# Keys of both kv heads in one transpose, doubled over the partitions by their stores (hybrid attention and convolution block, one core)

## The chip, the cores and the metric

The kernel runs on one core of one Trainium2 chip. The metric is the device time of one execution in microseconds. Shown with the kernel are three timed runs and one execution taken by the hardware profiler. Engines are named as in the profile: PE is TensorE's matmul, PEld its weight load, DVE is VectorE, ACT is ScalarE, POOL is GpSimd, and SP is SyncE, which issues the DMAs.

## What is computed

One encoder layer over two sequences (256 and 2048 tokens), each with the same 16 meta tokens in front. Every token row is normalised, multiplied with one input matrix, and the columns go two ways: a windowed attention with 8 query heads and 2 key/value heads, and a gated convolution. Both are gated, concatenated, multiplied with the output matrix and added to the input. What the change touches is the key part:

```python
h = rmsnorm(z, norm_w)
proj = jnp.einsum('bld,de->ble', h, w_in)
q, k, v, g_att, c_val, c_glu, g_conv = jnp.split(proj, SPLIT_IDX, axis=-1)
q = rmsnorm(q.reshape(B, L, N_HEADS, HEAD_DIM), q_norm_w)
k = rmsnorm(k.reshape(B, L, N_KV_HEADS, HEAD_DIM), k_norm_w)      # 2 heads of 64
att = windowed_gqa(q, k, v, sink).reshape(B, L, W_ATT) * jax.nn.silu(g_att)
cnv = conformer_conv(c_val, c_glu, conv_w, conv_b, ln_w, ln_b) * jax.nn.silu(g_conv)
return z + jnp.einsum('ble,ed->bld', jnp.concatenate([att, cnv], axis=-1), w_out)
```

In the attention a block of 128 queries sees its own block of keys, the two neighbours and the meta keys; the first and the last block of a sequence have one neighbour.

## The kernel before

Tokens come in 18 blocks of 128 (two of the short sequence, sixteen of the long one) and one small block of the 16 meta tokens, called block -1. Products run in single-pass fp32 (F32R) with each operand split into a high and a low part, so one product is three matmuls.

**Projection.** The input matrix is cut into 11 units of 256 columns, the tokens into 6 groups of 384 (400 with the meta tokens). Groups 0 to 2 form the first chunk and 3 to 5 the second. Within a chunk the units run in a fixed order: convolution, its gate, attention gate, then keys and values (unit 8), then queries (units 6 and 7). So keys are made twice, once for blocks -1 to 8 and once for blocks 9 to 17. `c_group` and `g_group` multiply by `proj_et` (L863); `kv_group` and `q_group` by `proj_te` (L879), where 24 matmuls of 256 columns fill one PSUM tile named `pj`. Results that the attention needs go to DRAM: `kd` and `kmd` (keys), `vd`, `qd`, `gd`, `cd`.

**One key block** (`kv_block`). ACT squares and sums the keys of each head, POOL makes the inverse root `rk`, DVE multiplies (`kn`, L1037). The score product later wants the 64 rows of a head twice, in partitions 0 to 63 and again in 64 to 127, since the queries `q2` stand there as high part and low part (`q_split`, L403 to L406). Before, DVE writes each head twice side by side, so `kn` has 256 columns, and PE transposes each head's 128 columns by itself (L1048, two transposes into one PSUM tile `kt`). ACT scales to the high part of `ks` (L1055, 256 columns), DVE makes the low part (L1056, 256 columns), and one store writes `ks` to `kd`.

**Attention.** `load_k` brings the keys of one block's window into one of two tiles `kw`: five DMAs for an inner block, one for a first or last block (L300). `scores` multiplies `q2` with `kw` (S, L383); then bias and maximum on DVE (L441), the exponential on ACT (L453), the normalisation on POOL, transposes (L499), the product with the values (O, L533) and the output projection (y, L609). The first blocks' attention steps are spread through the last query units (`spread`), where a query block is first copied out of PSUM by ACT (`qr`, L1004), squared (`sqq`, L980), and multiplied on DVE much later (L1010); its buffer comes free when its store to `qd` has landed.

**What sets the order.** Steps are written out by a clock of ticks: `later(k, f)` runs `f` after k ticks, `store` issues a DMA two ticks later, and convolution steps on DVE (L946) are drawn by a credit of time. Beneath that a scheduler places the instructions of each engine by its own cost table, except in stretches that are marked manual (POOL from the opening of the attention, PE too after the last query block). All DMAs are issued by SP, in order. Each carries one of eight completion semaphores in turn, and its issue waits for the DMA that carried the same one, eight issues before.

Of the kernel before, what the change touches and what calls it, by code (L numbers as in the profile page):

```python
# [18 lines left out]
P = 128  # L19
D = 1024  # L20
ND = D // P
NM = 16
# [77 lines left out]
def hymba_kernel(  # L100
# [19 lines left out]
    kd = dram.tile([P, 2, KV, TOK], F32, name="kd")  # L120
    kmd = dram.tile([P, 2, KV, NM], F32, name="kmd")
# [15 lines left out]
    km = const.tile([P, 2, KV, NM], F32R, name="km")  # L137
# [56 lines left out]
    def store(dst, src):  # L194
        later(2, lambda: nc.sync.dma_start(dst, src))
# [59 lines left out]
    def attention_open():  # L255
# [10 lines left out]
        for i in range(2):  # L266
            kw.append(ap.tile([P, 2, KV, KW], F32R, tag=f"kw{i}", name=f"kw{i}", bufs=1))
# [27 lines left out]
    def load_k(b):  # L295
        t = kw[b % 2].bitcast(F32)
        at = P * (b - 1)
        if kind(b) != "in":
            at += P * (kind(b) == "first")
            nc.sync.dma_start(t[:, :, :, CC:MB], kd[:, :, :, at : at + 2 * P])  # L300
            return
        nc.sync.dma_start(t[:, :, :, CC:LB], kd[:, :, :, at + P : at + 2 * P])
        nc.sync.dma_start(t[:, :, :, LA:MA], kd[:, :, :, at : at + QC])
        nc.sync.dma_start(t[:, :, :, LB:RA], kd[:, :, :, at + QC : at + P])
        nc.sync.dma_start(t[:, :, :, RA:MB], kd[:, :, :, at + 2 * P : at + 2 * P + QC])
        nc.sync.dma_start(t[:, :, :, RB:KW], kd[:, :, :, at + 2 * P + QC : at + 3 * P])
# [103 lines left out]
    def scores(b, kv, n):  # L410
# [13 lines left out]
        for hl_k in range(2):  # L424
# [4 lines left out]
                kw[b % 2][:, hl_k, kv, c0:c1],  # L429
# [271 lines left out]
    if True:  # L701
# [321 lines left out]
        def kv_block(ws, g, o, rows, b):  # L1023
# [8 lines left out]
            kn = sp.tile([P, KV, 2, HD], F32, tag="kn", name=f"kn{b}")  # L1032
            owe(800)

            def fin():
# [3 lines left out]
                    pk.unsqueeze(2).to_broadcast([rows, KV, 2, HD]),  # L1039
                    rk[:rows, :KV].unsqueeze(2).unsqueeze(3).to_broadcast([rows, KV, 2, HD]),  # L1040
# [4 lines left out]
            def fin2():  # L1045
                pt = psum.tile([P, 512], F32, tag="d", name=f"kt{b}")
                for kv in range(KV):
                    nc.tensor.transpose(  # L1048
                        pt[:, P * kv : P * kv + rows],
                        kn[:rows, kv].rearrange("p a e -> p (a e)"),  # L1050
                        ident[:rows, :rows],
                    )
                ks = sp.tile([P, 2, KV, P], F32R, tag="ks", name=f"ks{b}")
                pr = pt[:, : 2 * P].rearrange("p (a n) -> p a n", n=P)[:, :, :rows]
# [265 lines left out]
```

## Time and profile before

| | us |
|---|---|
| three timed runs | 948.51, 948.61, 950.12 |
| median | 948.61 |
| the profiled execution | 947.32 |
| its span in the profile | 945.3 |
| PE busy in it | 938.1 |
| DVE, ACT, POOL busy | 748.8, 424.1, 296.7 |

Times in the profile count from the span's start. A row of a timeline has the start, the length, the engine, the line, the operation with its tiles, the count and, in brackets, idle time before it with what ended it. The length of a PE row is modelled to its drain, so rows overlap; the step from one start to the next is what a matmul takes of PE.

### The profile page before, as it was taken

What the parts mean: (1) busy time and instruction counts of PE and PEld (TensorE: products, weight loads), DVE (VectorE), ACT (ScalarE), POOL (GpSimd) and SP (SyncE); (2) the same over time, 40 slices, a digit from 0 to 9 for tenths busy, and PEclk for the clock granted to TensorE, in tenths of its full rate; (3) what the DMA queues carried; (4) which work ended last, traced back from release to release, by engine and by line L of the source; (5) the groups of instructions that cost most, each with busy time, mean ns of one, the idle gap of its engine ahead of it and who ended that gap; (6) DMA issues with size and microseconds to landing.
All of it is one profiled execution on the core that took longest, in us unless ns stands there. A gap on an engine that the chain in (4) does not pass through costs nothing.

```text
span 945.3 us, 16681 instructions
## 1 busy us (share of the span) xinstructions
PE 938.1 (99%) x5813; PEld 887.7 (94%) x5813; DVE 748.8 (79%) x1263; ACT 424.1 (45%) x1160; POOL 296.7 (31%) x490
## 2 busy tenths in 40 slices
PE   8999999999999999999999999999999999999998
PEld 8999999999999999999999999988888888888887
DVE  5579999997987879999995655687777677767763
ACT  7432022253457751011111456566666566656661
POOL 4310000183478400000000453755433243333332
PEclk9999999999999999999999999999999999999999
DMA  8585345686556595223333496985666556655512
GB/s 305 169 275 193 134 176 176 222 277 236 159 187 190 187 328 175 89 111 135 140 130 123 138 353 189 398 260 156 197 188 174 152 162 192 187 164 143 165 64 67
DMA packets 148659, 176.49 MB, mean 187 GB/s; under 512 B 40704, under 2 KB 111184, under 8 KB 148448
## 3 DMA queue, kind: packets, MB, share of 16 engines
q1 hardware_dynamic: 148576, 175.43, 57.4%
q8 instruction: 46, 0.75, 0.3%
q14 instruction: 37, 0.30, 0.1%
HBM read 112.69 MB, written 62.70 MB: 186 GB/s over the span
## 4 chain that ended last, share of the span: by engine, by line
PE 85%; DMA 5%; DVE 4%; SPq 2%; POOL 1%; ACT 1%; issue 1%; DVEq 0%; POOLq 0%; ACTq 0%
PE pj L863 41%; PE y L609 21%; PE pj L879 8%; PE O L533 5%; PE S L383 4%; PE pT_c L499 2%; PE pT_m L499 2%; PE pT_x L499 1%; DMA kw<-kd 1%; DMA qd<-qr 1%; DVE xt L772 1%; DVE y L946 1%; PE qT L383 1%; DMA cd<-zn 1%; DMA wraw<-in_w_in 1%
## 5 line engine op out<-in xcount | busy, mean ns | idle before, releaser
L863 PE MATMUL pj<-xh,ws 128*128 128x384 f32 (+1 forms) x1536 | 395.9, 338 | 0.1
L946 DVE SCALAR_TENSOR_TENSOR y<-us,cw,y 128x1167 f32<-128x1167 f32 x240 | 329.0, 1428 | 0.4
L863 PEld LDWEIGHTS pj<-xh,ws 128*128 128x128 f32 x1536 | 280.0, 188 | 0.4 <-ACT xh L1116 0.4
L863 PE MATMUL pj<-xl,ws 128*128 128x384 f32 (+1 forms) x768 | 260.8, 340 | 0.1
L609 PE MATMUL y<-wo,rest 128*128 128x512 f32 (+1 forms) x672 | 173.2, 395 | 0.0
L879 PE MATMUL pj<-ws,xh 128*128 128x256 f32 (+1 forms) x880 | 165.8, 284 | 0.9 <-ACT sqq L980 0.5
L863 PEld LDWEIGHTS pj<-xl,ws 128*128 128x128 f32 x768 | 144.1, 188 | 0.5 <-DVE xl L801 0.4
L879 PEld LDWEIGHTS pj<-ws,xh 128*128 128x128 f32 (+1 forms) x880 | 136.5, 187 | 2.3 <-ACT sqq L980 0.8
L609 PEld LDWEIGHTS y<-wo,rest 128*128 128x128 f32 x672 | 117.5, 189 | 21.7 <-DVE rest L566 0.3
L879 PE MATMUL pj<-ws,xl 128*128 128x256 f32 (+1 forms) x440 | 124.3, 283 | 0.0
L441 DVE CUSTOM_DVE_ANT_0 sb<-S,bias,vec 128x304 f32<-128x304 f32 (+5 forms) x144 | 74.4, 517 | 32.2 <-PE S L383 31.4
L453 ACT ACTIVATE sb<-sb,nm 128x304 f32<-128x304 f32 (+5 forms) x144 | 77.8, 541 | 48.9 <-DVE nm L441 48.2
L971 ACT ACTIVATE go<-pj 128x384 f32<-128x384 f32 x48 | 23.5, 490 | 149.8 <-PE pj L863 138.3
L879 PEld LDWEIGHTS pj<-ws,xl 128*128 128x128 f32 (+1 forms) x440 | 82.2, 187 | 0.2
L561 POOL TENSOR_TENSOR at<-at,ga 128x256 f32<-128x256 f32 x36 | 26.5, 735 | 164.8 <-DVE at L555 105.1
L479 POOL TENSOR_SCALAR sb<-sb,es 128x304 f32<-128x304 f32 (+5 forms) x144 | 73.1, 526 | 16.0 <-DVE es L466 13.2
L148 POOL TENSOR_SCALAR ssk<-ssk 128x2 f32<-128x2 f32 x18 | 7.5, 419 | 213.1 <-ACT sqk L985 211.1
L383 PEld LDWEIGHTS S<-kw,q 128*128 128x128 f32 x288 | 53.2, 188 | 11.3 <-issue 0.3
L383 PE MATMUL S<-kw,q 128*128 128x304 f32 (+5 forms) x288 | 62.7, 299 | 0.2 <-issue 0.2
L148 POOL TENSOR_SCALAR ssq<-ssq 128x4 f32<-128x4 f32 (+2 forms) x55 | 26.4, 479 | 96.5 <-ACT xn L726 73.6
L906 ACT ACTIVATE sg<-pj 128x384 f32<-128x384 f32 (+1 forms) x24 | 11.8, 492 | 83.1 <-PE pj L863 66.1
L609 PE MATMUL y<-wo,mch 128*128 128x512 f32 x144 | 47.2, 409 | 0.0
(139 smaller groups left out, 1317.7 us busy)
## 6 DMA issues: line engine op xcount, KB each, us to landing
wd<-ws SPq DMA_DIRECT2D x36, 512.0 KB, 6.0
ws<-wd SPq DMA_DIRECT2D x36, 512.0 KB, 6.0
wraw<-in_w_in SPq DMA_DIRECT2D x52, 256.0 KB, 6.4
xn<-in_z SPq DMA_DIRECT2D x18, 512.0 KB, 5.5
gd<-go SPq DMA_DIRECT2D x48, 192.0 KB, 2.1
yo<-in_z SPq DMA_DIRECT2D x36, 256.0 KB, 3.9
out_y<-yo SPq DMA_DIRECT2D x35, 256.0 KB, 2.6
wo<-wod SPq DMA_DIRECT2D x16, 512.0 KB, 7.5
```

The lines of the kernel that those rows point to most:

```text
L148: nc.gpsimd.tensor_scalar(src, src, scale, eps, op0=ALU.mult, op1=ALU.add)
L383: r = f(*a, **k)
L441: nc.vector.tensor_tensor_reduce(out=sb[:, n, c0:c1], in0=ps[:, 0:w], in1=cst["bias"][:, kv, at + c0 : at + c1], scale=1.0, scalar=nsnk[:, ...
L453: nc.scalar.activation(sb[:, n, c0:c1], sb[:, n, c0:c1], AF.Exp, bias=nm[:, n : n + 1], scale=-1.0, accum_out=rs[:, n : n + 1],)
L479: nc.gpsimd.tensor_scalar(sb[:, k, a0:a1], sb[:, k, a0:a1], es[:, k : k + 1], 1.0, op0=ALU.mult, op1=ALU.mult)
L499: nc.tensor.transpose(pt[: c1 - c0, n, :], sbt[b, kv][:, n, c0:c1], ident)
L533: nc.tensor.matmul(opj[b, kv][:, n0:n1], t[:r, kv, :], p[:r, n0:n1], start=(k == "c" and i == 0), stop=(k == "x" and i == len(work) - 1),)
L561: nc.gpsimd.tensor_tensor(at[:, pr, :], at[:, pr, :], gat[b][:, pr, :], op=ALU.mult)
L609: nc.tensor.matmul(ps, mh[mi][:, e % 4, :], wo[e, wi][:, cols], start=(e == 4 and k == 0), stop=(e == 3 and k == 2),)
L863: nc.tensor.matmul(ps[:, :n], ws[:, d, wi, P * half_i : P * half_i + P], x[xi][:, d, o : o + n], start=(k == 0), stop=(k == 3 * ND - 1),)
L879: nc.tensor.matmul(ps[:rows, :UW], x[xi][:, d, o : o + rows], ws[:, d, wi, :], start=(k == 0), stop=(k == 3 * ND - 1),)
L946: nc.vector.scalar_tensor_tensor(y[:, yo + o0 : yo + o1], u[:, o0 + k : o1 + k], cw[:, j, k : k + 1], y[:, yo + o0 : yo + o1], op0=ALU.mul ...
```

## The change

The two heads of a key block are left side by side, 128 columns in all, and one transpose turns both: head 0 lands in partitions 0 to 63 and head 1 in 64 to 127. ACT and DVE then work on 128 columns instead of 256, for the meta block on 16 instead of 32. The doubling over the partitions is done by the store: one store per head, which reads 64 partitions of `ks` twice, by a stride of zero, and writes both halves of the DRAM tile. For that `kd` has a layout by block, in which a partition's row holds a head's high and low part side by side; `kw` and `km` swap their two middle dimensions to fit, and the first and last blocks of a sequence load their two key blocks with two DMAs.

```diff
-    kd = dram.tile([P, 2, KV, TOK], F32, name="kd")
-    kmd = dram.tile([P, 2, KV, NM], F32, name="kmd")
+    kd = dram.tile([NB, P, KV, 2, P], F32, name="kd")
+    kmd = dram.tile([P, KV, 2, NM], F32, name="kmd")
...
         t = kw[b % 2].bitcast(F32)
-        at = P * (b - 1)
         if kind(b) != "in":
-            at += P * (kind(b) == "first")
-            nc.sync.dma_start(t[:, :, :, CC:MB], kd[:, :, :, at : at + 2 * P])
+            at = b - (kind(b) == "last")
+            for k in range(2):
+                nc.sync.dma_start(t[:, :, :, CC + P * k : CC + P * k + P], kd[at + k])
             return
-        nc.sync.dma_start(t[:, :, :, CC:LB], kd[:, :, :, at + P : at + 2 * P])
+        nc.sync.dma_start(t[:, :, :, CC:LB], kd[b])
...
-                kw[b % 2][:, hl_k, kv, c0:c1],
+                kw[b % 2][:, kv, hl_k, c0:c1],
...
-            kn = sp.tile([P, KV, 2, HD], F32, tag="kn", name=f"kn{b}")
+            kn = sp.tile([P, KV, HD], F32, tag="kn", name=f"kn{b}")
...
                 nc.vector.tensor_tensor(
                     kn[:rows],
-                    pk.unsqueeze(2).to_broadcast([rows, KV, 2, HD]),
-                    rk[:rows, :KV].unsqueeze(2).unsqueeze(3).to_broadcast([rows, KV, 2, HD]),
+                    pk,
+                    rk[:rows, :KV].unsqueeze(2).to_broadcast([rows, KV, HD]),
                     op=ALU.mult,
                 )
...
+                nc.tensor.transpose(pt[:, :rows], kn[:rows].rearrange("p a e -> p (a e)"), ident[:rows, :rows])
+                ks = sp.tile([P, 2 * P], F32R, tag="ks", name=f"ks{b}")
+                nc.scalar.mul(ks[:, :rows], pt[:, :rows], kscale[:, 0:1])
+                nc.vector.scalar_tensor_tensor(
+                    ks[:, rows : 2 * rows], pt[:, :rows], kscale[:, 0:1], ks[:, :rows], op0=ALU.mult, op1=ALU.subtract
+                )
+                to = (kmd if b < 0 else kd[b]).rearrange("(h p) k l n -> p h k (l n)", h=2)
                 for kv in range(KV):
-                    nc.tensor.transpose(
-                        pt[:, P * kv : P * kv + rows],
-                        kn[:rows, kv].rearrange("p a e -> p (a e)"),
-                        ident[:rows, :rows],
-                    )
-                ks = sp.tile([P, 2, KV, P], F32R, tag="ks", name=f"ks{b}")
-                pr = pt[:, : 2 * P].rearrange("p (a n) -> p a n", n=P)[:, :, :rows]
-                nc.scalar.mul(ks[:, 0, :, :rows], pr, kscale[:, 0:1])
-                nc.vector.scalar_tensor_tensor(
-                    ks[:, 1, :, :rows], pr, kscale[:, 0:1], ks[:, 0, :, :rows], op0=ALU.mult, op1=ALU.subtract
-                )
-                store(
-                    kmd if b < 0 else kd[:, :, :, P * b : P * b + P], ks[:, :, :, :rows].bitcast(F32)
-                )
+                    part = ks[HD * kv : HD * kv + HD, : 2 * rows].bitcast(F32)
+                    store(to[:, :, kv, :], part.unsqueeze(1).to_broadcast([HD, 2, 2 * rows]))
```

The lines after `fin2` stand five lower in the changed file (the transpose is L1047, ACT's scaling L1049, DVE's low part L1050). The cost table knows the shorter instructions, so the scheduler places others anew around the keys and up to the end of the last query unit.

On PE, in the second chunk's key unit, before: `pj` is the projection's PSUM tile, `kt` the transposed keys of one block, x2 a row of two equal instructions.

```order
L879 MATMUL pj_5439<-ws_8_4916,xl_3485 128x256
L879 MATMUL pj_5439<-ws_8_4916,xh_3484 128x256 x2
L879 MATMUL pj_5439<-ws_8_4916,xl_3485 128x256
L1048 MATMUL kt_5430<-ident,kn_5370 128x128 x2
L879 MATMUL pj_5439<-ws_8_4916,xh_3484 128x256 x2
L879 MATMUL pj_5439<-ws_8_4916,xl_3485 128x256
```

The same place on PE in the changed kernel:

```order
L879 MATMUL pj_5437<-ws_8_4916,xl_3485 128x256
L879 MATMUL pj_5437<-ws_8_4916,xh_3484 128x256 x2
L879 MATMUL pj_5437<-ws_8_4916,xl_3485 128x256
L1047 MATMUL kt_5429<-ident,kn_5368 128x128
L879 MATMUL pj_5437<-ws_8_4916,xh_3484 128x256 x2
L879 MATMUL pj_5437<-ws_8_4916,xl_3485 128x256
```

One of the pair is gone; it is so in all 18 blocks and in the meta block, and nothing is added on PE.

On ACT, where the first attention block's queries are prepared, before: `qr_9` is a query block on its way out of PSUM, `zn` the layer norm of the convolution, `q_0` the split queries that the first scores read.

```order
L243 ACTIVATE zn_5914<-lnu_5965,vec 128x128 x4
L1004 COPY qr_17_6139<-pj_6114 128x256
L1004 COPY qr_9_6191<-pj_6166 128x256
L243 ACTIVATE zn_5974<-lnu_6024,vec 128x128 x4
L403 CAST q_0_6040<-qT_6035 64x4x4x32
L404 CAST q_0_6040<-qT_6035 64x4x4x32
```

The same place on ACT in the changed kernel:

```order
L1004 COPY qr_17_6141<-pj_6116 128x256
L243 ACTIVATE zn_5915<-lnu_5966,vec 128x128 x4
L243 ACTIVATE zn_5975<-lnu_6025,vec 128x128 x4
L403 CAST q_0_6041<-qT_6036 64x4x4x32
L404 CAST q_0_6041<-qT_6036 64x4x4x32
L1004 COPY qr_16_6067<-pj_6042 128x256
L980 ACTIVATE sqq_16_6070<-pj_6042 128x256
L980 ACTIVATE sqq_17_6144<-pj_6116 128x256
L243 ACTIVATE zn_6034<-lnu_6079,vec 128x128 x4
L1004 COPY qr_9_6193<-pj_6168 128x256
```

The copy of `qr_9` stood ahead of the two casts of `q_0`, and now stands seven instructions behind them (the four of `zn` share a row).

On SP, near the end of the query units, before: `kw` is a key load of an end block, `qd<-qr_9` the store of that query block.

```order
L329 DMA q_6717<-qd 128x512
L364 DMA ga_6753<-gd 128x4x128
L300 DMA kw_5835<-kd 128x4x256
L195 DMA qd<-qr_9_6191 128x256
L195 DMA qd<-qr_10_6245 128x256
```

The same place on SP in the changed kernel:

```order
L329 DMA q_6720<-qd 128x512
L364 DMA ga_6756<-gd 128x4x128
L300 DMA kw_5835<-kd 128x4x128 x2
L195 DMA qd<-qr_9_6193 128x256
L360 DMA wo_6581<-wod 128x1024
```

Ahead of the store of `qr_9` there are two key loads of half the size in place of one.

12 lines of the change are left out of this document (6 added, 6 removed).

## The prediction

> **What bounds the kernel now.** I read the page first, the span and the engines' busy time.
>
> ```profile
> span 945.3 us, 16681 instructions
> PE 938.1 (99%) x5813; PEld 887.7 (94%) x5813; DVE 748.8 (79%) x1263; ACT 424.1 (45%) x1160; POOL 296.7 (31%) x490
> ```
>
> PE never rests: 7.2 us of the span are idle on it (945.3 less 938.1). So the time is the sum of PE's steps and its few stalls; work taken from DVE or ACT is worth nothing by itself. The profiled execution took 947.32 us, its span is 945.3, so 2.0 us lie outside. I make the sum against 947.32 and carry the difference to the median of the runs, 948.61.
>
> Next, what PE waits for: the view of waits on PE, less its two rows of the first 30 us, which the change doesn't reach.
>
> ```profile
> PE pj L879 <- ACT sqq L980: 0.5, 1, 0.5
> PE pj L879 <- DVE qs L1010: 0.3, 1, 0.3
> PE S L383 <- issue: 0.2, 1, 0.2
> ```
>
> Three stalls, all in the query units just behind the keys. Then the stages, as busy time by windows (start and end; PE, PEld, DVE, ACT, POOL; granted clock, DMA share, GB/s):
>
> ```profile
> 220.00:245.00 25.00, 25.00 (x213) 24.53 (x212) 23.68 (x39) 9.30 (x48) 10.67 (x18) 1.00 0.58 190
> 570.00:586.00 16.00, 15.85 (x136) 15.67 (x135) 7.76 (x20) 10.52 (x29) 6.13 (x14) 1.00 0.48 158
> 586.00:604.00 18.00, 18.00 (x153) 17.82 (x151) 9.88 (x33) 9.62 (x32) 11.90 (x25) 1.00 1.03 360
> 615.00:945.00 330.00, 327.18 (x1825) 282.13 (x1824) 237.70 (x617) 196.87 (x508) 127.42 (x215) 1.00 0.56 162
> ```
>
> The clock is full everywhere. In the first chunk's key unit (220 to 245) DVE is nearly full too; from 586 to 604 the DMA engines are. From 615 on PE is busy 327.18 of 330 us, in an order that the change leaves alone: what is won before 615 moves the end.
>
> **The transposes: the main term.** What the key blocks cost now is shown by the view of the tile `kt` (count; shortest, median, longest in ns), and what one transpose takes of PE by a place where one stands alone between projection matmuls (timeline of PE):
>
> ```profile
> L1048 PE MATMUL kt<-ident,kn x36: 270/272/300, 233.7 to 546.0; 128*128 128x128 f32 x36
> ...
> 285.05 0.28 PE L879 MATMUL pj<-ws,xh 128*128 128x256 f32 x1
> 285.17 0.27 PE L221 MATMUL lnt<-ident,y 128*128 128x128 f32 x1
> 285.20 0.36 PE L879 MATMUL pj<-ws,xh 128*128 128x256 f32 x1
> 285.40 0.28 PE L879 MATMUL pj<-ws,xl 128*128 128x256 f32 x1
> ```
>
> A `pj` hands over after 0.12 (285.05 to 285.17). From the `pj` before the transpose to the second behind it are 0.35 us (285.05 to 285.40), of which two steps of `pj` are 0.24: the transpose costs 0.11. A pair of `kt`:
>
> ```profile
> 528.95 0.29 PE L879 MATMUL pj<-ws,xh 128*128 128x256 f32 x1
> 529.07 0.38 PE L1048 MATMUL kt<-ident,kn 128*128 128x128 f32 x2
> 529.21 0.37 PE L879 MATMUL pj<-ws,xh 128*128 128x256 f32 x1
> 529.41 0.28 PE L879 MATMUL pj<-ws,xl 128*128 128x256 f32 x1
> ```
>
> 0.46 less 0.24 is 0.22, again 0.11 each: a pair has no share that a single one keeps. 36 become 18, and the meta block's two become one: 19 times 0.11 is **2.09 us** off PE, which nothing hid. The bounds are this and 0.2 more: half a hundredth of rounding for each, and the meta block's unlike shape.
>
> The Trainium skill ("TensorE: Matmul & The Clock Gate", Part 4: PE-mode transpose) gives about 275 ns for a transpose within a kernel, mostly access latency. The row of `kt` has the same 272 ns, but as the length of an instruction and not as its step; taken as the price, the skill's figure would make 5.2 us of the 19 instead of 2.1; the steps of 0.11 speak against reading it so.
>
> **DVE and ACT.** The nearest rows for 128 columns are the value split's, beside the keys' (count; sum in us, mean ns):
>
> ```profile
> L1056 DVE SCALAR_TENSOR_TENSOR ks<-kt,kscale,ks 128x256 fp32r<-128x256 f32 x18 | 8.6, 479 | 0.3 <-ACT ks L1055 0.3
> L1055 ACT ACTIVATE ks<-kt,kscale 128x256 fp32r<-128x256 f32 x18 | 8.6, 475 | 10.3 <-PE kt L1048 7.4 <-DMA kd<-ks 2.8
> L1037 DVE TENSOR_TENSOR kn<-pj,rqk 128x256 f32<-128x256 f32 x18 | 7.6, 421 | 4.0 <-POOL rqk L149 4.0
> L1029 DVE TENSOR_TENSOR vs<-pj,vs 128x128 fp32r<-128x128 f32 x18 | 5.0, 284 | 11.5 <-ACT vs L1028 11.3 <-issue 0.2
> L1028 ACT CAST vs<-pj 128x128 fp32r<-128x128 f32 x18 | 4.6, 261 | 0.0
> ```
>
> DVE saves 18 x (421 + 479 - 2 x 284) ns = 6.0 us, ACT 18 x (475 - 261) ns = 3.9 us. PE waits for neither in the key units, so these count at nothing there. They can count at one stall behind:
>
> ```profile
> 264.48 0.28 PE L879 MATMUL pj<-ws,xh 128*128 128x256 f32 x1
> 265.04 0.35 PE L879 MATMUL pj<-ws,xh 128*128 128x256 f32 x1 [0.28 <-DVE qs L1010]
> ...
> 260.47 0.41 DVE L981 TENSOR_REDUCE ssq<-sqq 128x4 f32<-128x256 f32 x1
> 264.47 0.42 DVE L1010 TENSOR_TENSOR qs<-pj,rqq 128x256 f32<-128x256 f32 x1 [0.90 <-POOL rqq L149]
> ```
>
> PE loses 0.44 us here (a step of 0.56 for 0.12), waiting for a PSUM tile that DVE frees after POOL's root, which waits for DVE's sum at 260.47, queued behind keys and convolution. A DVE that is some microseconds ahead makes that sum earlier. The gain lies between 0 and 0.44; I take half, **0.22**.
>
> **The first scores.** The second stall, with its chain on ACT and DVE:
>
> ```profile
> 580.24 0.28 PE L879 MATMUL pj<-ws,xl 128*128 128x256 f32 x1
> 580.67 0.43 PE L383 MATMUL S<-kw,q 128*128 128x176 f32 x2 [0.15 <-issue]
> ...
> 576.16 0.37 ACT L1004 COPY qr<-pj 128x256 f32<-128x256 f32 x1 [4.36 <-DMA qd<-qr]
> 577.81 0.58 ACT L403 CAST q<-qT 64x512 fp32r<-64x512 f32 x1
> 579.72 0.69 DVE L406 TENSOR_TENSOR q<-qT,q 64x512 fp32r<-64x512 f32 x1
> ```
>
> ACT stood 4.36 us for the buffer of a query copy, whose old content was still on its way to DRAM, and the casts of the first queries stood behind. DVE ended its half at 580.41, and PE lost 0.31 us (0.43 for 0.12). By the order given with the change the copy now stands behind the casts, so the casts no longer wait for a store. What would be late next is the layer norm ahead of the casts, which reads nothing but PE's transposes. I take the whole **0.31** off; the bounds are that and nothing.
>
> **The DMAs.** Stores of keys go from one of 256 KB to two of 128 KB. The rows of the view of DMA issues (count, KB each, us to landing):
>
> ```profile
> kd<-ks SPq DMA_DIRECT2D x18, 256.0 KB, 2.6
> vd<-vs SPq DMA_DIRECT2D x18, 128.0 KB, 2.4
> ```
>
> The buffer `ks` comes back when the second store has landed: 2.4 plus an issue of about 0.5, so 0.3 later than 2.6. ACT waits for that buffer at a few blocks (2.8 us in all, row L1055 above), and it would wait 5.4 more if all 18 grew by 0.3. Behind it in ACT's queue stand the squares and value copies of the next block, which free a `pj` tile; PE has four of these in turn in the key unit and shows no stall there. So I cost it at nothing; where that cover is gone, a block costs its 0.3.
>
> The end blocks' loads, cut in two, stand before something PE does wait for, the third stall:
>
> ```profile
> 603.98 0.27 PE L499 MATMUL pT_m<-ident,sb 128*128 128x128 f32 x1
> 604.76 0.39 PE L879 MATMUL pj<-ws,xh 128*128 128x256 f32 x1 [0.52 <-ACT sqq L980]
> ...
> 604.05 0.37 ACT L1004 COPY qr<-pj 128x256 f32<-128x256 f32 x1 [2.94 <-DMA qd<-qr]
> ...
> 597.50 6.53 DMA qd<-qr
> ...
> 596.23 0.57 SPq L300 DMA_DIRECT2D kw<-kd  x1
> 597.50 1.61 SPq L195 DMA_DIRECT2D qd<-qr  x2
> ```
>
> The store of `qr_9`, issued at 597.50, lands 6.53 us later, ACT's copy starts at 604.05, and PE goes on at 604.76 with 0.67 us lost (a step of 0.78 for a transpose's 0.11). The store now stands behind two loads instead of one, of the same bytes. With the DMA engines full (1.03 from 586 on) it is the bytes in front that set the landing, so the delay is near nothing; the second issue costs 0.57 at most by the row of `kw`. A later issue by one whole step of this stretch (596.23 to 597.50: 1.3 us) is a rival. I take **0.2** added, nearer to the bytes' end.
>
> Sum: -2.09 - 0.22 - 0.31 + 0.20 = -2.42. 947.32 becomes 944.9, and the median 948.61 becomes **946.2**, 0.26% less. A measurement of this kernel can tell about 0.2%, or 1.9 us, from no change: the border stands at 946.7.
>
> **The rivals.** *The gain ends at the join.* If the DMA stream that ends in the store of `qr_9` doesn't start earlier when PE does, PE merely waits 2.1 us longer at 604.76. For: the stream is full from 586 on, and ACT's wait there is 2.94 already. Against: between 570 and 586 the DMA engines are busy for 0.48 only, so that stretch is paced by what PE frees. Time: 948.6, no change. Chance 0.12.
>
> *The split loads take a step each.* Three of the four end loads fall between 547 and 604, where SP's issue waits for a landing eight issues before. If each of the three added issues holds SP for a whole step of 1.3 us, and the stores behind land later by that, the two joins at 580 and 604 lose 3.9 us, with the 0.2 above 4.1, against the 2.1 won: 948.61 + 2.0 = 950.6. It decides from the second step on, since two take 2.6. For: SP's steps of 1.3 us in the rows above. Against: a landing after 6.53 us at the window's 360 GB/s means that over 2 MB lie ahead in the queue, so that a later issue starves no DMA engine, and the same bytes land by the same time. Chance 0.06.
>
> *A transpose costs its length.* If PE's real saving is 0.272 each, 19 make 5.2 and the median would be 948.61 - 5.2 - 0.3 = 943.1. Against: the steps of 0.11 in both timelines. The Trainium skill's section on PE-mode transposes, named above, gives this time too if its figure is read as a price. Chance 0.03.
>
> **How the numbers follow.** My forecast has the remaining 0.79, with a range of its own from 944.9 (2.09 + 0.2 won, both stalls of 0.44 and 0.31 gone, nothing added, and 0.7 for the spread of runs, of which the three shown span 1.6) to 947.4 (2.09 less 0.9 of new stalls, since the scheduler has put other instructions around the keys too). Of it 0.60 lie below 946.7 and 0.19 above. Faster: 0.60 + 0.03 = 0.63. Slower, above 950.5: half of the second rival, 0.03. The rest, 0.34, is the same. The range has to reach into the first rival to hold 8 in 10: 944.9 to 948.4.
>
> **What would show it right or wrong.** PE's rows: `kt` 18 times and the span near 942.9; a step of 0.35 us from the `pj` before one `kt` to the second `pj` behind it. The rows at the first S without a stall, and the casts of `q` no more behind a wait for `qd<-qr`. At the last query block a stall between 0.6 and 1.2 us; 2.8 there would be the first rival, and S stalled for over 1.5 as well the second. DVE busy about 6 us less, ACT about 4. I'd be wrong if PE has new stalls of over a microsecond in the query units, or if the steps around single transposes aren't 0.11.

## The result, and the profile after

The changed kernel takes 944.07 us, the median of four runs (943.38 to 944.83). The kernel before took 948.78 beside it (four runs, 948.51 to 950.12). The ratio is 0.9948, 95% interval 0.9930 to 0.9965: faster by 4.7 us, where 2.4 were forecast and the range ended at 944.9. The profiled executions lie 3.4 us apart, 943.95 and 947.32.

The first lines of the page of the changed kernel:

```profile
span 941.9 us, 16665 instructions
PE 935.6 (99%) x5794; PEld 886.3 (94%) x5794; DVE 744.4 (79%) x1263; ACT 421.8 (45%) x1160; POOL 293.3 (31%) x490
```

PE has 19 instructions fewer, as it should, and the span is 3.4 us shorter where 2.4 were forecast. DVE has 4.4 us less and ACT 2.3. Next, what PE waits for (engine, line, releaser; us in all, times, longest), less the two rows of the first microseconds:

```profile
PE lnu L240 <- DVE zn L234: 0.7, 1, 0.7
PE pj L879 <- DVE kn L1037: 0.3, 1, 0.3
```

The three stalls that the prediction spoke of are gone, and two stand in new places. The first is in the key unit of the first chunk. Timelines of PE, DVE and POOL:

```profile
254.32 0.28 PE L879 MATMUL pj<-ws,xh 128*128 128x256 f32 x1
254.86 0.36 PE L879 MATMUL pj<-ws,xh 128*128 128x256 f32 x1 [0.26 <-DVE kn L1037]
...
252.28 1.43 DVE L946 SCALAR_TENSOR_TENSOR y<-us,cw,y 128x1167 f32<-128x1167 f32 x1
...
254.43 0.28 DVE L1037 TENSOR_TENSOR kn<-pj,rqk 128x128 f32<-128x128 f32 x1
...
252.50 1.77 POOL L149 TENSOR_TENSOR rqk<-ssk,half 128x2 f32<-128x2 f32 x1
```

PE loses 0.42 us (a step of 0.54 for 0.12) until DVE has read a key block out of PSUM. DVE comes to it at 254.43, without a gap behind the convolution step, a low half of values and a split of weights; the root that it needs is on POOL until 254.27. The second stands before a layer norm's transposes, just ahead of the first scores; timelines of PE, DVE and ACT:

```profile
574.29 0.28 PE L879 MATMUL pj<-ws,xh 128*128 128x256 f32 x1
575.22 0.63 PE L240 MATMUL lnu<-ident,zn 128*128 128x128 f32 x4 [0.66 <-DVE zn L234]
...
574.27 0.81 DVE L234 TENSOR_SCALAR zn<-lnt,mv 128x512 f32<-128x512 f32 x1 [4.00 <-DMA cd<-zn]
...
572.72 0.58 ACT L403 CAST q<-qT 64x512 fp32r<-64x512 f32 x1
...
574.60 0.37 ACT L1004 COPY qr<-pj 128x256 f32<-128x256 f32 x1 [0.71 <-PE pj L879]
```

The casts now stand ahead of the query copy, as the order said. But DVE has waited 4.00 us for the buffer of an earlier `zn`, whose store to `cd` landed only at 574.14, and PE loses 0.82 (0.93 for 0.12).

To see where the 3.4 us went, I cut both timelines of PE at six places that both kernels have: the meta block's first transpose, the first gated matmul of the second chunk, the second chunk's first `kt`, the first S, the first output product with a low half, and the end of the last matmul. Before (its first S stands in the prediction, at 580.67):

```profile
230.56 0.29 PE L1048 MATMUL kt-1_2119<-ident,kn-1_2075 16*128 16x16 f32 x2
...
304.87 0.34 PE L863 MATMUL pj<-xh,ws 128*128 128x384 f32 x1
...
520.73 0.38 PE L1048 MATMUL kt<-ident,kn 128*128 128x128 f32 x2
...
609.66 0.39 PE L609 MATMUL y<-wo,mcl 128*128 128x512 f32 x1
...
939.67 2.51 PE L609 MATMUL y<-wo,rest 128*128 128x512 f32 x16
```

After:

```profile
230.47 0.23 PE L1047 MATMUL kt-1_2119<-ident,kn-1_2075 16*128 16x16 f32 x1
...
303.23 0.34 PE L863 MATMUL pj<-xh,ws 128*128 128x384 f32 x1
...
518.97 0.27 PE L1047 MATMUL kt<-ident,kn 128*128 128x128 f32 x1
...
578.41 0.36 PE L383 MATMUL S<-kw,q 128*128 128x176 f32 x2
...
606.89 0.39 PE L609 MATMUL y<-wo,mcl 128*128 128x512 f32 x1
...
934.75 3.94 PE L609 MATMUL y<-wo,rest 128*128 128x256 f32 x26
```

| stretch | before | after | change | forecast |
|---|---|---|---|---|
| start to the keys | 230.56 | 230.47 | -0.09 | 0 |
| keys and queries of the first chunk | 74.31 | 72.76 | -1.55 | -1.32 (ten transposes, half a stall) |
| on to the second keys | 215.86 | 215.74 | -0.12 | 0 |
| second keys to first S | 59.94 | 59.44 | -0.50 | -1.30 (nine transposes, the 0.31) |
| first S to low product (the join) | 28.99 | 28.48 | -0.51 | +0.20 |
| attention to the last matmul's end | 332.52 | 331.80 | -0.72 | 0 |
| on to the end of the span | 3.1 | 3.2 | +0.1 | 0 |

Two stretches together hold more than the profile's whole surplus of 1.0: 0.72 in the attention, of which I had said nothing, and 0.71 at the join (0.51 won where 0.20 was to be lost). The 1.3 us between the profiles' difference and that of the medians is still to be found.

### The profile page after: what moved, and what is told of

It is laid out like the page before. It is cut to its first block, busy times and chain, and to the rows that moved or that the text cites. A ratio compares the mean times of both kernels' runs of the same rounds, so it can differ in the third digit from the quotient of the medians.

```text
span 941.9 us, 16665 instructions
## 1 busy us (share of the span) xinstructions
PE 935.6 (99%) x5794; PEld 886.3 (94%) x5794; DVE 744.4 (79%) x1263; ACT 421.8 (45%) x1160; POOL 293.3 (31%) x490
## 4 chain that ended last, share of the span: by engine, by line
PE 94%; DMA 2%; DVE 1%; SPq 1%; issue 0%; ACT 0%; POOL 0%; DVEq 0%; ACTq 0%; POOLq 0%
PE pj L863 43%; PE y L609 21%; PE pj L879 13%; PE O L533 5%; PE S L383 4%; PE pT_c L499 2%; PE pT_m L499 2%; PE pT_x L499 1%; DMA cd<-zn 1%; DMA bias<-in_bias_c 1%; PE qT L383 1%; PE lnu L240 0%; DMA xn<-in_z 0%; PE lnt L221 0%; DVE xt L772 0%
## 5 line engine op out<-in xcount | busy, mean ns | idle before, releaser
L148 POOL TENSOR_SCALAR ssq<-ssq 128x4 f32<-128x4 f32 (+2 forms) x55 | 23.5, 427 | 98.3 <-ACT xn L726 74.4
```

Source lines behind the costliest of these rows:

```text
L148: nc.gpsimd.tensor_scalar(src, src, scale, eps, op0=ALU.mult, op1=ALU.add)
```

## The experiments

Numbers with an interval are ratios to the kernel before, run on the same chip. Where a stretch is named, it is cut as in the table.

**Both kernels again.** No edit. Before:

> The kernel before, once more, unchanged, for a second profile and its spread. Theory A (the extra gain is partly the spread of the kernel before: its profiled execution, 947.32, lay 1.3 us under its median of 948.6, so the profile that the sum was made against was a lucky one): ratio 1.000 within 0.002, the same stalls on PE at the same places (0.44 near 264.5, 0.3 near 294.5, 0.3 near 580.2, 0.7 near 604), and a span of the new profile between 945.3 and 948, the difference lying in stretches without a stall. Theory B (the kernel before takes 945.3 of span whenever it is profiled, and the change itself gave 4.7): a span within 0.3 of 945.3 again.

Ratio 0.9998 (0.9986 to 1.0009); the new profile has a span of 946.0. The stalls stand where they were, except that of 580, which is not there. The 0.7 us more come from the way to the keys, which takes 231.56 in place of 230.56, less 0.3 for that stall; all other stretches agree within 0.02. The start shows what made it longer: ten warm-up matmuls (L1101) take 2.50 us here, from 6.67 on, and 1.38 in the first profile, from 6.20 on. Theory A holds in that the time lies in no stall that the change touches; that the first profile was lucky at its start is not so, as the other profiles show below. After:

> The changed kernel once more, unchanged, beside the others of this call. All theories: ratio 0.995 within 0.0015. Its attention, from the first output product with a low weight half to the last matmul: 331.5 us as in its first profile, if that stretch is settled by the program and not by chance. The stall of 0.82 before the layer norm's transposes near 574 comes back at that place if the order makes it, and with another size if the landing of DMAs makes it.

Ratio 0.9957 (0.9945 to 0.9970): 944.33 against 948.37, 4.0 us. The attention is the same to 0.05 (331.56, counted as in the expectation). The stall near 574 is there with 0.28 in place of 0.82, so the order gives its place. Its size is the distance of two streams: the store of `zn` lands at 574.13, as in the first profile (574.14), while PE comes there 0.52 us later (574.81 for 574.29). The new stall in the first key unit comes back with 0.42. Start to keys is 231.26, with the long warm-up matmuls again (2.50 us for ten). Of all 17 profiles of this case three have these, with 231.3 to 231.6 to the keys; in the other 14 the ten take 1.38 and the keys begin at 230.4 to 230.6.

**Each transpose twice.**

```diff
                 nc.tensor.transpose(pt[:, :rows], kn[:rows]..., ident[:rows, :rows])
+                nc.tensor.transpose(pt[:, P : P + rows], kn[:rows]..., ident[:rows, :rows])
```

> The changed kernel with each of its 19 key transposes done twice, the second time into columns of the same PSUM tile that nobody reads: PE's work as before, everything else as in the changed kernel. Theory A (a transpose costs a step of 0.11 us): 2.1 us slower than the changed kernel, 946.2, give or take 1 us for stalls that the scheduler's new order makes or ends; two transposes take 0.22. Theory C (a transpose costs 0.25 to 0.27, which would give the measured 4.7 by itself): 4.7 to 5.2 us slower, 948.8 to 949.3, no gain left. Theory D (all of the gain came from stalls that shorter VectorE and ScalarE work ended): 944.1, no change.

Ratio 0.9988 (0.9979 to 0.9997), 0.3% or 2.9 us behind the changed kernel's 0.9957. Its price per transpose can be read off the timelines. A single one in the changed kernel, then a pair here:

```profile
245.36 0.28 PE L879 MATMUL pj<-ws,xh 128*128 128x256 f32 x1
245.48 0.27 PE L1047 MATMUL kt<-ident,kn 128*128 128x128 f32 x1
245.51 0.36 PE L879 MATMUL pj<-ws,xh 128*128 128x256 f32 x1
245.71 0.28 PE L879 MATMUL pj<-ws,xl 128*128 128x256 f32 x1
```

```profile
522.96 0.28 PE L879 MATMUL pj<-ws,xl 128*128 128x256 f32 x1
523.08 0.38 PE L1047 MATMUL kt<-ident,kn 128*128 128x128 f32 x2
523.22 0.48 PE L879 MATMUL pj<-ws,xh 128*128 128x256 f32 x2
523.54 0.28 PE L879 MATMUL pj<-ws,xl 128*128 128x256 f32 x1
```

From the `pj` ahead to the second behind are 0.35 us, 0.11 more than two steps. Behind the pair the third `pj` starts 0.58 after the one ahead, 0.22 more than three steps of 0.12. So 19 cost 2.1. The rest of the distance, 0.8 by the runs and 0.6 by the spans (944.6 to 941.9), is the balance of the stalls: in its profile the join has 0.88 and the first S 0.90, and the 0.42 in the first key unit is not there, where the changed kernel's has this, 0.82 ahead of the first S and none at the join. Theory C falls, since a gain is left; D falls, since not all of it is.

**DVE and ACT at their old length.**

```diff
-            kn = sp.tile([P, KV, HD], F32, tag="kn", name=f"kn{b}")
+            kn = sp.tile([P, 2, KV, HD], F32, tag="kn", name=f"kn{b}")
...
-                nc.scalar.mul(ks[:, :rows], pt[:, :rows], kscale[:, 0:1])
+                nc.scalar.mul(ks[:, :, :rows], pr, kscale[:, 0:1])
```

(`pr` is `pt[:, :rows]` read twice by a stride of zero; DVE's two instructions likewise.)

> The changed kernel with one transpose per block, but VectorE's two instructions on keys and ScalarE's one again over 256 columns (the added 128 are copies that nobody reads): only the shortening on VectorE and ScalarE is undone. Theory A: the stalls behind the first chunk's keys (0.44, 0.26 and 0.30 us in the profile before) come back at least in part, 0 to 1 us slower than the changed kernel, 944.1 to 945.1. Theory D: it loses the greater part of the gain, 946.5 or more. If the shortening is worth nothing: 944.1.

Ratio 0.9961 (0.9948 to 0.9975), which can't be told from the changed kernel's. The profile says more: the first chunk's keys and queries take 74.32, as long as before, though ten transposes are gone. The 1.55 went into stalls, of which one loses 1.22 (a step of 1.33 or 1.34 for 0.12):

```profile
254.41 0.28 PE L879 MATMUL pj<-ws,xh 128*128 128x256 f32 x1
255.74 0.36 PE L879 MATMUL pj<-ws,xh 128*128 128x256 f32 x1 [1.05 <-DVE kn L1037]
...
252.62 1.44 DVE L946 SCALAR_TENSOR_TENSOR y<-us,cw,y 128x1167 f32<-128x1167 f32 x1
253.96 1.30 DVE L839 TENSOR_TENSOR ws<-wraw,ws 128x512 fp32r<-128x512 f32 x2
...
252.85 2.97 POOL L149 TENSOR_TENSOR rqk<-ssk,half 128x2 f32<-128x2 f32 x1
```

In both profiles DVE has no gap ahead of `kn` (it starts at 255.17 here); `kn` stands behind other work. That this kernel loses only 0.4 us by the runs, and 0.8 by the spans (942.7 to 941.9), is the doing of the stretch up to the first S, which takes 58.34 in place of 59.44, without the stall near 574; the join has 0.17. So Theory A is right by the time and about the 0.44 near 264.5, which is back, and too modest about the first chunk; D fails by the time.

With the kernel before (74.31) and the doubled transposes (73.54) the first chunk's keys and queries can be told apart: shorter DVE and ACT work with the old number of transposes wins 0.77, ten fewer transposes with the old lengths win nothing, and both together 1.55. The schedules differ, so this is no exact division; but there the transposes' 1.10 depend on the shortening.

**The split loads alone**, put into the kernel before:

```diff
-            nc.sync.dma_start(t[:, :, :, CC:MB], kd[:, :, :, at : at + 2 * P])
+            for k in (0, P): nc.sync.dma_start(t[:, :, :, CC + k : CC + k + P], kd[:, :, :, at + k : at + k + P])
```

> The kernel before with the end blocks' key loads cut in two, as the change has them, and nothing else; the order on every engine but SyncE is that of the kernel before. The prediction's term: 0.2 us slower, the stall near 604 grows from 0.67 to about 0.87. The rival of the split loads: up to 3.9 us slower, with both stalls near 580 and 604 longer by 1.3 us and more. A third way, which the profile after suggests since its stall near 604 is gone: the split loads cost nothing there, and the stall stays at 0.67 because the store of the query copy lands at the same time.

Ratio 1.0007 (0.9997 to 1.0018). Near the join, rows of SP and of PE:

```profile
598.94 1.80 SPq L300 DMA_DIRECT2D kw<-kd  x2
601.54 1.57 SPq L195 DMA_DIRECT2D qd<-qr  x2
...
605.54 0.27 PE L499 MATMUL pT_m<-ident,sb 128*128 128x128 f32 x1
607.56 0.38 PE L879 MATMUL pj<-ws,xh 128*128 128x256 f32 x1 [1.75 <-ACT sqq L980]
```

The store of `qr_9` is issued 2.60 us behind the first key load, where it was 1.27 (596.23 to 597.50): the second load holds the queue for a step of 1.3, as the rival had it. The join's stall is 1.91 in place of 0.67, and 1.5 us more are lost before the first S (61.47 for 59.94). The runs are only 0.5 us slower, with an interval that holds 1, so this profile is an unlucky one. That the split costs the kernel before something is likely all the same: none of its 12 runs is under 948.3, and 12 of the 29 of the kernel before beside it are.

**The new layout alone**, with the old work:

```diff
-                store(
-                    kmd if b < 0 else kd[:, :, :, P * b : P * b + P], ks[:, :, :, :rows].bitcast(F32)
-                )
+                store(kmd if b < 0 else kd[b], ks[:, :, :, :rows].bitcast(F32))
```

(with `kd`, `kmd`, `kw`, `km`, `load_k` and the S product as in the change.)

> Only the new order of keys in DRAM and in SBUF, with the end blocks' loads in two, and all of the old work: VectorE doubles the keys, two transposes per block, one store of 256 KB. Theory E (the key layout by itself shortens the attention): from the first output product with a low weight half to the last matmul 331.5 us as in the three kernels with the new layout, not the 332.2 of the three with the old, and by rounds 0.7 us less than the kernel before plus what the split loads cost (0.5 by the rounds of that kernel): about 948.2. Theory F (the shorter attention comes from something else in the change): 332.2 there, and 948.9 by rounds.

Ratio 1.0011 (1.0000 to 1.0023), but its attention is 331.56: Theory E. In this profile the loss is at the join, 2.38 us there, and 0.68 at the first S, and then there is a second price. A row of PE and a window behind the join (columns as in the prediction, the granted clock third from the end):

```profile
607.60 0.57 PE L879 MATMUL pj<-ws,xh 128*128 128x256 f32 x1 [2.21 <-ACT sqq L980]
...
607.65:611.06 3.41, 3.41 (x16) 3.41 (x17) 3.38 (x12) 3.16 (x10) 0.00 (x0) 0.50 1.01 395
```

For 3.41 us behind the stall the granted clock is 0.50, and the 16 matmuls from 607.60 on take 3.53 us, where they took 2.00 in the profile before (604.76 to 606.76): 1.5 more. Five of the 12 runs have a mean clock of 0.998 or 0.996 and take 950.7 to 951.8; the other seven take 947.6 to 950.5, with a median of 948.5. So most of what the ratio adds to the expected 948.2 comes from these five.

**Where the layout acts.** Its SBUF half and its DRAM half apart, each in the kernel before:

```diff
-            kw.append(ap.tile([P, 2, KV, KW], F32R, tag=f"kw{i}", name=f"kw{i}", bufs=1))
+            kw.append(ap.tile([P, KV, 2, KW], F32R, tag=f"kw{i}", name=f"kw{i}", bufs=1))
...
-                kw[b % 2][:, hl_k, kv, c0:c1],
+                kw[b % 2][:, kv, hl_k, c0:c1],
...
```

> The kernel before with one thing of the change: a key's high and low half lie side by side for each kv head in the tile kw (and in km and the DRAM copies, whose token axis stays whole), so that the two S products of a head read columns 416 apart instead of 832. Every instruction, DMA and order as in the kernel before. Theory E1 (the shorter attention comes from where TensorE reads the keys in SBUF): the stretch from the first output product with a low weight half to the last matmul is 331.5 us in place of 332.2, and by rounds the kernel is 0.7 faster than the one before, ratio 0.9993. Theory E2 (it comes from the key blocks in DRAM, through the DMAs that run beside the attention): 332.2 and ratio 1.000.

```diff
-    kd = dram.tile([P, 2, KV, TOK], F32, name="kd")
+    kd = dram.tile([NB, P, 2, KV, P], F32, name="kd")
...
```

> The kernel before with the other half of the new layout: key blocks apart in DRAM and the end blocks' loads in two; the tile kw keeps its old order. Theory E1: attention 332.2, and by rounds 0.5 us slower than before, as the kernel with the split loads alone (948.9). Theory E2: attention 331.5, 948.2. By the step of the rival of the split loads the store of the query copy near 604 is issued 2.6 us behind the first key load in place of 1.3 in both cases.

The first low product and the last matmuls, by PE's timelines of the SBUF half and the DRAM half, in this order:

```profile
611.12 0.39 PE L609 MATMUL y<-wo,mcl 128*128 128x512 f32 x1
...
939.75 3.22 PE L609 MATMUL y<-wo,rest 128*128 128x256 f32 x20
```

```profile
611.21 0.40 PE L609 MATMUL y<-wo,mcl 128*128 128x512 f32 x1
...
939.78 3.94 PE L609 MATMUL y<-wo,rest 128*128 128x256 f32 x26
```

From the start of the one to the end of the other are 331.85 and 332.51 us, where the table has 332.52 before and 331.80 after (the expectations count to the start of the last matmul, 0.28 less). E1 is shown as far as the place goes: the order of the keys in SBUF does it, with no instruction moved. (The DRAM copies swap their middle dimensions along with it; the padded kernels below leave DRAM as it was.) But it is not the products that read the keys which get shorter. Summed as steps from one start to the next, the attention's S products take 41.67 us in the kernel before and 41.74 in the SBUF half, the products with the values 48.21 and 48.06, the output products 208.07 and 207.48. By the runs the SBUF half is 0.9997 (0.9988 to 1.0007), which holds the 0.9993 expected and 1 as well: its profile loses 1.55 us at the first S and the join and wins 0.67 behind them. The DRAM half is 1.0014 (1.0003 to 1.0024), its store issued a second step late too.

**More buffers** for the query copies and for `zn`, in both kernels:

```diff
-                    raw = gp.tile([P, 4, HD], F32, tag="go" if b % 2 else "qs", name=f"qr{qi}_{b}")
+                    raw = gp.tile([P, 4, HD], F32, tag="qr", name=f"qr{qi}_{b}", bufs=6)
...
-            st["zn"] = yp.tile([P, 512], F32, tag="zn", name=f"zn{b}", bufs=3)
+            st["zn"] = yp.tile([P, 512], F32, tag="zn", name=f"zn{b}", bufs=4)
```

> The changed kernel with six buffers of their own for the query copies of the last units and four instead of three for the layer norm's tile: the waits for stores of these are taken away. Theory G (what is left of PE's stalls between 560 and 610 are waits for those landings): PE stands less than 0.3 us there in place of 0.82 and more, 0.8 to 1.0 us faster than the changed kernel, ratio about 0.9942. If other waits take their place (loads of keys, sums on VectorE): no change, 0.995.

> The kernel before with the same added buffers. Theory G: its stalls near 580 and 604 (0.31 and 0.67) go, 1.0 us faster than the kernel before, ratio 0.999; beside the changed kernel with the same buffers it then shows the change without the joins: transposes 2.1, attention 0.7, stalls behind the first chunk's keys 0.5, together 3.3 us. If the luck of the joins made the surplus of the gain, the two lie 2.1 us apart and no more.

Changed: 0.9963 (0.9951 to 0.9976), no gain; a wait of 0.4 for DVE, near 604.5, takes their place. Before: 0.9993 (0.9985 to 1.0002); its stalls at 580 and 604 go, and two of 0.6 for the attention's tiles come near 607. Its 11 runs lie close, 947.31 to 948.52, where the 23 of the kernel before reach from 946.68 to 950.22. So the waits for landings make a good part of that spread. Between the two with more buffers lie 2.9 us by the runs and 3.6 by the spans (945.3 and 941.7), near the 3.3 expected: of the gain of 4.0 to 4.7, some 3 don't hang on the joins. For the joins' own share the intervals leave anything from nothing to some 3 us.

**Whole loads in the changed kernel**, at the price of four stores:

```diff
-                    store(to[:, :, kv, :], part.unsqueeze(1).to_broadcast([HD, 2, 2 * rows]))
+                    for h in (0, HD): store(to[h : h + HD, kv], part)
...
```

> The changed kernel with its end blocks' loads whole again (keys lie in DRAM with one token axis), for which each block's keys go out in four stores of 64 KB in place of two of 128. If the split loads cost the changed kernel something at the joins (the prediction's 0.2, or a step of 1.3 each by its rival), this is 0.2 to 1.3 us faster, 943.0 to 944.1, with the store of the query copy issued 1.3 us behind the key load and not 2.6. If the second load's step is hidden there: 944.3, no change, or slower by what the 38 more store issues cost on the queue in the key units (0.3 us for each that nothing covers).

Ratio 1.0038 (1.0024 to 1.0052), nearly 8 us behind the changed kernel. The store of `qr_9` is issued 1.33 behind the key load, but the join had nothing to win: first S to low product takes 28.57, against 28.48 with the loads in two. So the second load's step is hidden in the changed kernel's profile. What makes the four stores so dear was not followed to its end; the profile has stalls of 2.2 us near 563 and 0.9 near 270 that no other kernel has, and behind the first the granted clock is 0.50 again, from 565.59 to 569.00.

**The keys moved apart.** Unused columns behind each row of `kw`, 16 or 32, in either kernel:

```diff
-            kw.append(ap.tile([P, 2, KV, KW], F32R, tag=f"kw{i}", name=f"kw{i}", bufs=1))
+            kw.append(ap.tile([P, 2, KV, KW + 16], F32R, tag=f"kw{i}", name=f"kw{i}", bufs=1))
```

> The kernel before with sixteen unused columns behind each of the four rows of the tile kw, so that the two S products of a head read columns 864 apart instead of 832; every instruction, DMA and order as in the kernel before. Theory H (any other place of the two key halves shortens the attention, the old distance of 832 was an unlucky one): from the first output product with a low weight half to the last matmul 331.5 us. Theory I (it needs the halves side by side): 332.2, as in the kernel before.

> The changed kernel with sixteen unused columns behind each of the four rows of the tile kw; nothing else differs. If the place of the keys in SBUF sets the attention's steps in the changed kernel too, the stretch from the first output product with a low weight half to the last matmul leaves 331.5 us, and with the gain of the padded kernel before it would be 331.2; 0.3 us less is the only way in which this could beat the changed kernel (944.0 in place of 944.3). If the change has already taken all there is: 331.5.

> The changed kernel with thirty-two unused columns behind each row of kw: the two halves of a head's keys lie 1792 bytes apart, a multiple of 256. Theory J (a distance between the two halves that is a multiple of 256 bytes is the slow one: 3328 in the kernel before is, 1664 and 3456 are not): the attention's stretch goes back to 332.2 us. Theory K (it isn't the distance): 331.5 or less.

> The kernel before with thirty-two unused columns behind each row of kw: the halves lie 3584 bytes apart, a multiple of 256. Theory J: the attention's stretch is 332.2 us as in the kernel before, while sixteen columns gave 331.2. Theory K: below 332.

Counted as the expectations do, the attention is 331.23 in the kernel before with 16 columns and 331.55 with 32, against 332.2; in the changed kernel 331.70 and 331.58, against 331.5. These are single profiles, and in the padded kernels the tiles behind `kw` may lie elsewhere too. With that said, H holds: the kernel before had the slowest place of all that were tried. Theory J falls, since both kernels with 32 columns are at 331.6. What in a place makes the steps longer, of products that don't read the keys above all, stays open. The changed kernel with 16 columns has a ratio of 0.9945 (0.9931 to 0.9960), not to be told from 0.9957, and its attention is not shorter: no version here is shown to beat the changed kernel.

**What the joins are worth.** In three of these kernels every engine runs the instructions of the kernel before in the same order (the SBUF half, and the two padded ones of before), and two have the order of the changed kernel. From the second chunk's first `kt` to the first low product, cut as in the table:

| order | us | mean |
|---|---|---|
| before: two profiles, SBUF half, 16 and 32 columns | 88.93, 88.65, 90.48, 91.50, 90.20 | 89.95 |
| after: two profiles, 16 and 32 columns | 87.92, 87.43, 86.98, 87.62 | 87.49 |

The means lie 2.46 apart, of which nine transposes make 0.99. The other 1.5 are waits for landings. That figure leans on the three variants: the two profiles of the kernel before and the two of the changed one lie 1.1 apart, which leaves 0.1 to the joins. The runs stand between: of their 4.0 to 4.7 the other stretches of the table and the nine transposes make 3.4 (1.55, 0.12, 0.72 and 0.99), which leaves 0.6 to 1.3. The profile that the prediction was made against, 88.93, is shorter than those of the three variants by 1.27 us and more. An unlucky one, the kernel before with 16 columns, PE and DVE:

```profile
573.62 0.28 PE L879 MATMUL pj<-ws,xh 128*128 128x256 f32 x1
575.24 0.66 PE L240 MATMUL lnu<-ident,zn 128*128 128x128 f32 x4 [1.33 <-DVE zn L234]
...
574.37 0.81 DVE L234 TENSOR_SCALAR zn<-lnt,mv 128x512 f32<-128x512 f32 x1 [2.93 <-DMA cd<-zn]
...
605.82 0.27 PE L499 MATMUL pT_m<-ident,sb 128*128 128x128 f32 x1
607.31 0.38 PE L879 MATMUL pj<-ws,xh 128*128 128x256 f32 x1 [1.22 <-ACT sqq L980]
```

The same instructions in the same order stand here 1.50 us for a `zn` and 1.38 at the join, where the profile before had none and 0.67.

## Why the prediction was right or wrong

The direction was right and the price of its main term, **the transposes**, was right to the hundredth: 0.11 each, 2.09 in all, singly and in pairs. That "nothing hid" them was right only together with the shorter work on DVE: with the old lengths the first chunk gave none of its 1.10 back. The gain was 4.0 to 4.7 us where 2.4 were forecast, because of three other terms.

**The attention** failed by its first step: "in an order that the change leaves alone: what is won before 615 moves the end". The order is indeed the same, and still the stretch is 0.7 us shorter in every kernel with the new order of keys in SBUF. I had followed the change in `kw` as bookkeeping and gave it no term, not even an unknown one with bounds. It is 0.7 of the 1.6 to 2.3 us by which the forecast fell short.

**The two joins**, "the first scores" and "the third stall", were sized from one execution. I took 0.31 off for the one and put 0.20 on for the other, -0.11 in all; the means of five and four profiles give -1.5, the runs -0.6 to -1.3, and how much it is stays open within that. The mechanism of the 0.31 was as written, the casts ahead of the copy, but that stall is not in the second profile before either. What was wrong is that the layer norm ahead of the casts "reads nothing but PE's transposes": DVE's `zn` waits for the buffer that a store to `cd` must free, and PE lost 0.82 and 0.28 there; with a fourth buffer for `zn` that stall is gone. The 0.20 had the wrong sign. The added load does hold the queue for 1.3 us, as "the split loads take a step each" had it, and with the old order the kernel pays: 1.91 at the join with the split loads alone. With the changed order it doesn't; the store of `qr_9` lands 22.4 us behind the first S there (ACT's copy at 600.78, S at 578.41), where it took 23.4 before (604.05 and 580.67):

```profile
592.83 1.86 SPq L300 DMA_DIRECT2D kw<-kd  x2
595.40 0.75 SPq L195 DMA_DIRECT2D qd<-qr  x1
...
600.78 0.37 ACT L1004 COPY qr<-pj 128x256 f32<-128x256 f32 x1 [1.66 <-DMA qd<-qr]
...
601.99 0.27 PE L499 MATMUL pT_m<-ident,sb 128*128 128x128 f32 x1
602.02 0.36 PE L879 MATMUL pj<-ws,xh 128*128 128x256 f32 x1
```

The key load is issued 14.4 us behind the first S, against 15.6, and PE does not stop. Why the stream of DMAs is ahead by that microsecond was not isolated; in the second profile after it is ahead by 0.1 to 0.2 only, and PE loses 0.27.

**The stall at 264.48** went whole, 0.44 and not half. Two smaller ones that I had not listed went too (0.31 near 294.5, 0.26 near 258.3), and one of 0.42 came at 254.32. "PE waits for neither in the key units, so these count at nothing there" was the wrong step: with the old lengths and the new order PE does wait for DVE, and without the shortening nothing is left of the 1.55 of that stretch. DVE's 23.68 busy us from 220 to 245, which the prediction showed, were the sign.

**DVE and ACT** saved 4.4 and 2.3 us, not 6.0 and 3.9. The value split's 284 and 261 ns were not the nearest price for an instruction that scales out of PSUM:

```profile
L1049 ACT ACTIVATE ks<-kt,kscale 128x128 fp32r<-128x128 f32 x18 | 6.6, 368 | 11.5 <-DMA kd<-ks 6.5 <-PE kt L1047 4.9
L1050 DVE SCALAR_TENSOR_TENSOR ks<-kt,kscale,ks 128x128 fp32r<-128x128 f32 x18 | 6.2, 345 | 1.7 <-ACT ks L1049 1.6
```

ACT's waits for the buffer `ks` grew from 2.8 to 6.5 us, and no stall of PE is put down to them: the stores in two cost nothing that shows, as said.

The sum, by means of profiles: -1.55 in the first chunk, -0.12 on the way, -2.46 to the low product, -0.71 in the attention, together -4.8. The two comparisons by runs give 4.7 and 4.0. Against the first profile alone it was 3.4, since that execution had short joins. Of the three rivals none came true as written; the third, with 943.1, came nearer to the measured time than the forecast, but by luck, since the step stayed at 0.11.

## What to carry to other kernels

A stall that ends with a DMA's landing has no size of its own: before one profile's stalls become terms of a sum, compare that execution with the median of the runs (here 947.32 with 948.6), and give such stalls bounds as wide as that difference. A change of layout that moves no instruction still moves where an operand lies, so it needs a term with bounds for each stretch that reads it. Work taken from an engine that is "not waited for" may pay in a stretch where that engine is nearly full, as DVE is in the key unit. And look at the granted clock behind a stall before you compare two executions: here two stalls of over 2 us were each followed by 3.41 us at half clock.

## What the runs showed of the hardware

The place of the key tile in SBUF moves the steps of the matmuls in the attention: with the same 1855 matmuls in the same order this stretch took 332.2 us (332.22 to 332.27) in the three kernels with the old place, and 331.2 to 331.7 in the ten with other places; the two that were profiled twice repeat it to 0.05. (The pair with more buffers, in which a few instructions lie otherwise, has 332.5 and 331.8.) The difference is in the output products and the products with the values (208.07 to 207.48 and 48.21 to 48.06 us in the SBUF half) and not in the S products, whose moving operand the keys are; it is spread, and no wait shows in the trace. The Trainium skill ("SBUF — State Buffer", section "Who interferes with whom") says that TensorE never waits on anyone at SBUF's ports. The runs don't show a wait on another engine, but they do show that the address of a tile counts; why is open.

Two long stalls of PE were each followed by a stretch at half clock. The stalls of 2.38 us at the join of the kernel with the new layout alone and of 2.2 us near 563 in the one with whole loads were the only ones of over 2 us behind the start, and each had a granted clock of 0.50 for 3.41 us behind it, which cost 1.5 us in the first; behind the next longest, 1.91 in the kernel with the split loads alone, the clock stayed at 1.00. Where between the two the border lies, and whether the length alone decides, was not tried. Runs of these kernels with a mean clock of 0.998 fit one such stretch (an estimate: half of 3.41 us in some 947 is 0.0018).

POOL's root of two columns, 0.70 us by its median in the changed kernel, is recorded with 1.77 beside a convolution step of DVE and with 2.97 where DVE went on without a gap, in the rows above. The same section says that a DVE instruction with two inputs in SBUF contends with a POOL instruction that reads SBUF; the rows agree, though spans on POOL are rough: the `kn` that reads the longer root starts at 255.17, before the root's recorded end of 255.82. That PE's new stall comes from this is not shown, since DVE had no gap ahead of `kn`, and in the profile before a root of 2.97 at 252.27 cost PE nothing.
